# Two fused transformer blocks, float32: seven-product groups in another order, two weight sums on VectorE, eight plain tiles first

## The chip, the core and the metric

The kernel runs on one core of a Trainium2 chip. The metric is device time in microseconds (us) of one launch. TensorE (PE in the profile) multiplies, VectorE (DVE) and ScalarE (ACT) do elementwise work, GpSimd (POOL) does elementwise work and issues the transfers that add into memory, SyncE (SP) issues the plain transfers. Each engine takes its own instructions strictly in program order.

## What is computed

Two blocks over 512 tokens of width 2048, with 16 meta tokens ahead of them in the first. All is float32. The part that the change touches is the first product of block 1:

```python
def hybrid_layer(x, gain, w_in, pool_w, pool_scale, w_attn_up, w_pool_up, w_out):
    h = rmsnorm(x, gain)
    zin = h @ w_in
    q, k, v, g_attn, u, g_pool, m_attn, m_pool = split(zin)
    ...
    merged = sigmoid(m_attn) * y_attn + sigmoid(m_pool) * y_pool
    return x + merged @ w_out
```

m_attn and m_pool are 32 tiles of 128 columns (tiles 48 to 79 of w_in). Their sigmoids are computed first of all and parked in DRAM (`smd`). Only these 32 tiles change their computation; everything after them (attention, pooling, the second block with two layers) keeps its instructions and their order on every engine.

## The kernel before

**Arithmetic.** Every float32 operand is split in a high part (a rounding copy) and a low part (the rest): weights in `wh` (a cast on ACT, L195) and `wl` (a subtraction on DVE, L196), activations in `xh`, `xl`. A product takes three matmuls: xh·wh, xl·wh, xh·wl.

**Weights.** A chunk is 128 x 1024 float32 (512 KB), loaded by SP into one of five `ws` buffers. `ahead` casts and subtracts chunks in a fixed sequence of jobs, always three chunks ahead of the one that TensorE is about to use: `chunk`, at the start of every body, emits the split of job c+3, and only then do the matmuls of job c and their evacuation follow. That is the order on ACT and DVE: the split of a job three places ahead stands in front of the evacuation of the present one.

**Plain tiles.** The first NP = 6 of the 32 tiles are computed as they are: two chunks and 48 matmuls of 512 columns each. Meanwhile two generators work beside them: `sums` (the RMS norm) and `build`. `build` makes, for each of eight pairs j of activation tiles, the differences that the groups need: two scalings on ACT (`xt`, L538), one subtraction on POOL and four small operations on DVE (`sa`, `sb`), then two splits (`sh` on ACT, `sl` on DVE). The numbers in its `yield 0, delay, 0` say after how many planned ns its next part may be emitted. Whatever is not emitted when the plain tiles end is emitted at once (`need`). Evacuating a plain tile is a scaling (`p`), a clamp (`sg`) on DVE, and three activations on ACT (the sigmoid).

**Groups.** The other 26 tiles go in 13 groups of two. A group has four weight blocks: b11 and b21 are the two halves (over the 2048 inputs) of its first tile, b12 and b22 those of its second. With sums of them and of the activations it takes seven products of 24 matmuls of 256 columns, where two plain tiles take 96 of 512 columns. The products are named p1, p2, q5, p3, p6, p7, q4. Four weight blocks are loaded; four further operands are made by adding a block from DRAM into a loaded buffer with a transfer that POOL issues (L173, `accum_op=ALU.add`): q5 and p6 and q4 add b12, b22, b21 one after the other into the buffer T1 of p1, each after the split that reads the buffer, and p7 adds b22 into its own. The products of two groups are interleaved; with ' for the group before, the order is p1 p7' p2 q5 q4' p3 p6. Each product accumulates into one of three PSUM regions: a (p1, p2), c (q5, p3), b (p6, p7, q4). After p1 its partial sum is copied out (`after1`, ACT L278), and so on; `after6`, `after7`, `after4` read region b on DVE, and the next product into b must wait for them. `after7` and `after4` end in a clamp on DVE and the three sigmoid activations on ACT.

Of the kernel before, what the change touches and what calls it, by code (L numbers as in the profile page):

```python
# [9 lines left out]
ALU = mybir.AluOpType  # L10
# [36 lines left out]
class Unit:  # L47
    def __init__(self, chunks, body):
        self.chunks = chunks
        self.body = body  # L50


class Job:

    def __init__(self, load=None, src=None, acc=None, last=True, half=False):
        self.load, self.src, self.acc, self.last, self.half = load, src, acc, last, half
        self.tile = None
        self.w = (load if load is not None else acc).shape[-1]  # L60


class Group:
# [6 lines left out]
class K:  # L70
# [61 lines left out]
    def run(self, plan):  # L132
        plan = self.expand(plan)
        self.jobs = []
        for u in plan:
            if isinstance(u, Unit):
                for c in u.chunks:
                    if not isinstance(c, Job):
                        c = Job(load=c[0], half=True) if isinstance(c, tuple) else Job(load=c)
                    self.jobs.append(c)  # L140
        self.ci = self.si = self.di = self.ai = self.raw = 0
        self.split_w = {}
        for u in plan:
            if isinstance(u, Unit):
                for cost in u.body():
                    self.clock += cost
                    self.poll()
            else:
                u()
        self.need(*list(self.gens))  # L150
# [12 lines left out]
                    self.nc.sync.dma_start(t[:, a:b], j.load[:, a:b])  # L163
            self.di += 1

    def add(self, n):

        while self.ai < min(n, self.di):
            j = self.jobs[self.ai]
            if j.acc is not None:  # L170
                if j.src is not None:
                    j.tile = j.src.tile
                self.nc.gpsimd.dma_start(j.tile[:, :j.w], j.acc, accum_op=ALU.add)  # L173
            self.ai += 1

    def ahead(self, n):
        n = min(n, len(self.jobs))
        while self.si < n:
            self.fetch(self.si + 1)
            self.add(self.si + 1)  # L180
            j = self.jobs[self.si]
            t, w = j.tile, j.w
            h = self.wp.tile([P, CH], F32R, tag="wh", bufs=H_BUFS, name="wh")
            if j.half:

                h3 = h.rearrange("p (k c) -> p k c", c=P)
                t3 = t[:, :w].rearrange("p (k c) -> p k c", c=64)
                self.nc.scalar.copy(h3[:, :, :64], t3)
                self.nc.vector.tensor_tensor(h3[:, :, 64:], t3, h3[:, :, :64].bitcast(F32), ALU.subtract)
                l = None  # L190
            else:
                l = self.wp.tile([P, CH], F32R, tag="wl", bufs=L_BUFS, name="wl")
                cuts = [0, 256, w] if self.si == 0 else [0, w]
                for a, b in zip(cuts, cuts[1:]):
                    self.nc.scalar.copy(h[:, a:b], t[:, a:b])  # L195
                    self.nc.vector.tensor_tensor(l[:, a:b], t[:, a:b], h[:, a:b].bitcast(F32), ALU.subtract)  # L196
                    if self.si == 0 and a == 0:
                        self.first()
            self.split_w[self.si] = (h, l)
            if j.last:  # L200
                self.raw -= 1
            self.si += 1
            self.add(self.si + 2)

    def chunk(self):
        self.ahead(self.ci + 1 + AHEAD)
# [6 lines left out]
    def expand(self, plan):  # L213

        out, left, mid = [], [], []
        for n, u in enumerate(plan):
            if isinstance(u, Group):
                p1, p2, q5, p3, p6, p7, q4 = self.products(u)
                l7, l4 = left or ([], [])
                out += [p1, *l7, *mid, p2, q5, *l4, p3, p6]  # L220
                left, mid = [[p7], [q4]], []
            elif left and isinstance(u, Unit) and n + 1 < len(plan) and isinstance(plan[n + 1], Group):
                mid.append(u)
            elif left:
                out += left[0] + [u] + left[1] if isinstance(u, Unit) else left[0] + left[1] + [u]
                left = []
            else:
                out.append(u)
        return out + [x for l in left for x in l]

    def products(self, g):
# [5 lines left out]
        nc = self.nc  # L237
        b11, b21, b12, b22 = g.b
        st = {}
        lo, mid, hi = g.cols  # L240
        lom = lo - g.meta
        job = {"p1": Job(load=b11, last=False), "p2": Job(load=b21), "p3": Job(load=b22), "p7": Job(load=b12, acc=b22)}
        job["q5"] = Job(src=job["p1"], acc=b12, last=False)
        job["p6"] = Job(src=job["p1"], acc=b22, last=False)
        job["q4"] = Job(src=job["p1"], acc=b21)

        def product(key, op, region, first, after):
            cols = slice(lom if key in ("p1", "p2", "p3", "p6") else lo, mid)
# [23 lines left out]
        wide, half = slice(0, mid - lom), slice(lo - lom, mid - lom)  # L272
        one, two = slice(lom, mid), slice(mid, hi)
        first_half = slice(lo, mid)

        def after1(a):
            st["s"], st["v"], st["y0"], st["y1"] = self.U("s15"), self.U("vw"), self.U("y0"), self.U("y1")
            nc.scalar.copy(st["s"][:, one], a[:, wide])  # L278

        def after2(a):  # L280
# [3 lines left out]
            nc.scalar.copy(st["s"][:, two], c[:, half])  # L284

        def after6(b):
            v = st["v"]
            nc.vector.tensor_tensor(v[:, one], b[:, wide], st["s"][:, one], ALU.add)  # L288
            nc.vector.tensor_tensor(st["y1"][:, one], st["c"][:, wide], v[:, one], ALU.subtract)

        def after7(b):
            v, s = st["v"], st["s"]
            nc.vector.tensor_tensor(v[:, two], b[:, half], s[:, first_half], ALU.add)
            nc.vector.tensor_tensor(st["y1"][:, two], s[:, two], v[:, two], ALU.subtract)
            g.evacs[1](st["y1"])

        def after4(b):
# [1 line left out]
            g.evacs[0](st["y0"])  # L299

        return (product("p1", "A11", "a", True, after1), product("p2", "A12", "a", False, after2),
                product("q5", "S1", "c", True, after5), product("p3", "S4", "c", False, lambda c: None),
                product("p6", "S2", "b", True, after6), product("p7", "S3", "b", False, after7),
                product("q4", "A22", "b", False, after4))

# [174 lines left out]
    def block1(self, plan):  # L480
        nc, i = self.nc, self.i
        self.X = [None] * KT
        st = {}
# [49 lines left out]
        def build(xts):  # L533

            for j in range(KT // 2):
                x0, x1 = xts[2 * j], xts[2 * j + 1]
                for n, x in ((0, x0), (1, x1)):
                    nc.scalar.activation(x[:, :NT], x[:, :NT], AF.Copy, scale=self.vcol(V_NG, 2 * j + n))  # L538
                yield 0, 900, 0
                a, b = self.U("sa"), self.U("sb")  # L540
                nc.vector.tensor_tensor(a[:, HALF:NT], x0[:, HALF:NT], x1[:, HALF:NT], ALU.subtract)
                nc.gpsimd.tensor_tensor(b[:, HALF:NT], x0[:, META:HALF], x0[:, HALF:NT], ALU.subtract)
                nc.vector.tensor_scalar(a[:, :META], x0[:, :META], -1.0, None, ALU.mult)
                nc.vector.tensor_tensor(a[:, META:HALF], a[:, HALF:NT], x0[:, META:HALF], ALU.subtract)
                nc.vector.tensor_tensor(b[:, :HALF], x1[:, :HALF], a[:, :HALF], ALU.add)
                yield 0, 1500, 0
                r = []
                for t in (a, b):
                    h, l = self.UR("sh"), self.UR("sl")
# [1 line left out]
                    r.append((h, l))  # L551
                X0, X1 = self.X[2 * j], self.X[2 * j + 1]
                self.XS.append({"A11": X0, "A12": X1, "A22": X1, "S1": r[0], "S2": r[0], "S3": r[1], "S4": r[1]})
                yield 0, 2000, 0

        X = self.X
        XS = self.XS = []
# [109 lines left out]

            return Unit(chunks, body)

        NP = 6  # L670
        plan.append(load)
        plan.append(self.pair_unit([wt(48), wt(49)], X, [ev_m(0), ev_m(1)], lo=META, kts=EVEN_ODD))
        for n in range(2, NP):
# [910 lines left out]
```

## Time and profile before

| | us or share |
|---|---|
| median of 3 runs (2726.71 to 2731.55) | 2729.45 |
| the profiled execution, whole | 2726.03 |
| its span, first to last instruction | 2724.3 |
| plain tiles: start to the first group's first matmul | 6.67 to 79.32 |
| 13 groups: to the first matmul of the next stage | 79.32 to 383.59 |
| TensorE's share of the chain that ended last | 88% |

The profile gives busy times of the engines, a chain of work traced back from the end, groups of instructions with their durations and what ended the idle time before them, and, for a stretch, the granted TensorE clock (1.00 is 2.4 GHz, 0.50 is 1.2 GHz). A matmul's end is modelled, so the start times of consecutive matmuls say more than the busy share.

### The profile page before, as it was taken

What the parts mean: (1) busy time and instruction counts of PE and PEld (TensorE: products, weight loads), DVE (VectorE), ACT (ScalarE), POOL (GpSimd) and SP (SyncE); (2) the same over time, 40 slices, a digit from 0 to 9 for tenths busy, and PEclk for the clock granted to TensorE, in tenths of its full rate; (3) what the DMA queues carried; (4) which work ended last, traced back from release to release, by engine and by line L of the source; (5) the groups of instructions that cost most, each with busy time, mean ns of one, the idle gap of its engine ahead of it and who ended that gap; (6) DMA issues with size and microseconds to landing.
All of it is one profiled execution on the core that took longest, in us unless ns stands there. A gap on an engine that the chain in (4) does not pass through costs nothing.

```text
span 2724.3 us, 36840 instructions
## 1 busy us (share of the span) xinstructions
PE 2663.6 (98%) x14558; PEld 2299.0 (84%) x14558; DVE 1465.9 (54%) x2057; ACT 1181.9 (43%) x2074; POOL 552.9 (20%) x625
## 2 busy tenths in 40 slices
PE   8699989999999999999999999999999999999997
PEld 7699989889999888888888888888888888888886
DVE  7555554444444443544466665366555666546734
ACT  6555543444444322234345554344344555334433
POOL 2111101112112220002202231133320223112223
PEclk9899999999999999999999999999999999999998
DMA  5599962222222234444432223233342222332322
GB/s 195 132 219 232 229 175 86 78 78 81 81 71 82 86 116 142 139 136 139 141 107 70 78 78 97 84 107 93 105 145 90 78 78 78 98 96 84 106 93 70
DMA packets 100285, 304.78 MB, mean 112 GB/s; under 512 B 10896, under 2 KB 15376, under 8 KB 100112
## 3 DMA queue, kind: packets, MB, share of 16 engines
q1 hardware_dynamic: 90448, 273.06, 30.9%
q0 software_dynamic: 7488, 27.27, 5.7%
q8 instruction: 114, 1.87, 0.3%
q10 hardware_dynamic: 2176, 2.10, 0.2%
q14 instruction: 59, 0.48, 0.1%
HBM read 281.41 MB, written 20.97 MB: 111 GB/s over the span
## 4 chain that ended last, share of the span: by engine, by line
PE 88%; DMA 3%; DVE 3%; ACT 3%; issue 1%; POOL 0%; DVEq 0%; SPq 0%; ACTq 0%; POOLq 0%
PE pm L332 75%; DMA ws<-w_in 3%; PE s L1441 2%; ACT wh L195 2%; DVE wl L196 1%; PE o L1495 1%; PE o L1411 1%; PE t L1388 1%; PE pm L263 1%; PE o L923 1%; PE pm L264 1%; PE pm L265 1%; PE z L880 1%; PE t L1477 1%; PE s L1355 1%
## 5 line engine op out<-in xcount | busy, mean ns | idle before, releaser
L196 DVE TENSOR_TENSOR wl<-ws,wh 128x1024 fp32r<-128x1024 f32 (+2 forms) x480 | 622.3, 1302 | 472.7 <-ACT wh L195 467.8
L332 PE MATMUL pm<-xh,wh 128*128 128x512 f32 (+1 forms) x2240 | 742.3, 359 | 7.4 <-ACT xh L503 7.4
L332 PE MATMUL pm<-xl,wh 128*128 128x512 f32 (+1 forms) x2240 | 736.2, 357 | 0.2 <-DVE xl L504 0.2
L332 PE MATMUL pm<-xh,wl 128*128 128x512 f32 (+1 forms) x2240 | 735.8, 356 | 0.0
L195 ACT CAST wh<-ws 128x1024 fp32r<-128x1024 f32 (+2 forms) x480 | 491.6, 1028 | 384.7 <-PE pm L332 246.2
L332 PEld LDWEIGHTS pm<-xh,wh 128*128 128x128 f32 x2240 | 398.5, 188 | 69.2 <-ACT xh L503 8.1
L332 PEld LDWEIGHTS pm<-xh,wl 128*128 128x128 f32 x2240 | 396.4, 188 | 64.3
L332 PEld LDWEIGHTS pm<-xl,wh 128*128 128x128 f32 x2240 | 395.8, 188 | 59.2 <-DVE xl L504 1.3
L332 PE MATMUL pm<-yh,wh 128*128 128x512 f32 (+1 forms) x544 | 207.9, 382 | 0.0
L332 PE MATMUL pm<-yl,wh 128*128 128x512 f32 (+1 forms) x544 | 206.7, 380 | 0.0
L332 PE MATMUL pm<-yh,wl 128*128 128x512 f32 (+1 forms) x544 | 206.6, 380 | 0.0
L443 ACT ACTIVATE sg<-sg 128x512 f32<-128x512 f32 x80 | 50.5, 632 | 278.3 <-DVE sg L442 278.3
L263 PE MATMUL pm<-sh,wh 128*128 128x256 f32 x416 | 119.0, 286 | 15.0 <-DVE vw L288 9.4
L332 PEld LDWEIGHTS pm<-yh,wl 128*128 128x128 f32 x544 | 102.1, 188 | 21.0
L332 PEld LDWEIGHTS pm<-yl,wh 128*128 128x128 f32 x544 | 102.3, 188 | 19.6
L332 PEld LDWEIGHTS pm<-yh,wh 128*128 128x128 f32 x544 | 102.2, 188 | 19.7
L264 PE MATMUL pm<-sl,wh 128*128 128x256 f32 x416 | 117.7, 283 | 0.0
L265 PE MATMUL pm<-sh,wl 128*128 128x256 f32 x416 | 117.4, 282 | 0.0
L263 PE MATMUL pm<-xh,wh 128*128 128x256 f32 x312 | 88.8, 285 | 22.6 <-ACT s L278 22.0
L1004 POOL TENSOR_TENSOR gs<-p,sg 128x512 f32<-128x512 f32 x32 | 41.6, 1301 | 293.7 <-ACT sg L445 259.3
L332 PE MATMUL pm<-mh,wl 128*128 128x512 f32 x256 | 101.0, 395 | 0.0
L332 PE MATMUL pm<-mh,wh 128*128 128x512 f32 x256 | 100.9, 394 | 0.0
(336 smaller groups left out, 4505.0 us busy)
## 6 DMA issues: line engine op xcount, KB each, us to landing
ws<-w_in SPq DMA_DIRECT2D x283, 512.0 KB, 3.7
ws<-w_out SPq DMA_DIRECT2D x96, 512.0 KB, 3.9
ws<-w_in POOLq DMA_DIRECT2D x52, 512.0 KB, 7.0
smd<-sg SPq DMA_DIRECT2D x32, 256.0 KB, 5.2
ws<-w_au SPq DMA_DIRECT2D x16, 512.0 KB, 3.6
sm<-smd SPq DMA_DIRECT2D x32, 256.0 KB, 3.9
ws<-w_pu SPq DMA_DIRECT2D x16, 512.0 KB, 3.5
xr<-xs SPq DMA_DIRECT2D x32, 256.0 KB, 4.3
```

The costliest lines, as they stand in the source:

```text
L195: self.nc.scalar.copy(h[:, a:b], t[:, a:b])
L196: self.nc.vector.tensor_tensor(l[:, a:b], t[:, a:b], h[:, a:b].bitcast(F32), ALU.subtract)
L263: mm(o, wh[:, sl], xh, start=first and n == 0, stop=False, skip_group_check=True)
L264: mm(o, wh[:, sl], xl, start=False, stop=False, skip_group_check=True)
L265: mm(o, wl[:, sl], xh, start=False, stop=n == nj - 1, skip_group_check=True)
L332: mm(ps, w[:, sl], x[:, lo:hi], start=s, stop=e)
L443: nc.scalar.activation(e[:, :n], e[:, :n], AF.Exp, scale=-1.0)
L880: mm(o[:nb, lo:lo + ZW[b2]], lhs, t[x], start=False, stop=b2 == b and x == 1, skip_group_check=True)
L923: mm(o[:, ZC0[b]:S], vv, am[b][y], start=n == 0 and b == 0, stop=n == 2 and b == 4, skip_group_check=True)
L1004: nc.gpsimd.tensor_tensor(gs[:, :S], p[:, :S], e[:, :S], ALU.mult)
L1355: mm(o, q, kk[0][:, k0:k0 + 256], start=True, stop=False)
L1441: mm(o, p[:, q], r[:, :w], start=x == 0, stop=x == 4)
```

## The change

The order of a group's products becomes p1 p7' p2 q4' q5 p6 p3. Loads are now four (b11 for p1, b21 for p2, b22 in T6 and b12 in T3, which the jobs p6 and p3 fetch). Two sums remain with POOL's transfers: b12 into T1 after p1's split (for q5), b21 into T1 after p6's split (for q4). Two are now additions on DVE (128 x 1024 float32): T1 += T6 after q5's split (for p6), T3 += T6 after p6's split (for p7). `after6` and `after3` write into y1 instead of a buffer of their own. NP becomes 8, so there are 12 groups. `build` yields shorter delays.

```diff
@@ ahead @@
-            self.fetch(self.si + 1)
-            self.add(self.si + 1)
             j = self.jobs[self.si]
-            t, w = j.tile, j.w
+            self.fetch(self.si + 1 + 2 * bool(j.after))
+            t, w = j.src.tile, j.w
...
-            if j.last:
-                self.raw -= 1
+            self.raw -= len(j.frees)
+            for x, y in j.after:
+                if isinstance(y, Job):
+                    self.nc.vector.tensor_tensor(x.tile[:, :w], x.tile[:, :w], y.tile[:, :w], ALU.add)
+                else:
+                    self.nc.gpsimd.dma_start(x.tile[:, :w], y, accum_op=ALU.add)
             self.si += 1
-            self.add(self.si + 2)
@@ expand @@
-                out += [p1, *l7, *mid, p2, q5, *l4, p3, p6]
+                out += [p1, *l7, *mid, p2, *l4, q5, p6, p3]
@@ products @@
-        job = {"p1": Job(load=b11, last=False), "p2": Job(load=b21), "p3": Job(load=b22), "p7": Job(load=b12, acc=b22)}
-        job["q5"] = Job(src=job["p1"], acc=b12, last=False)
-        job["p6"] = Job(src=job["p1"], acc=b22, last=False)
-        job["q4"] = Job(src=job["p1"], acc=b21)
+        p1, p2, p6, p3 = Job(load=b11), Job(load=b21), Job(load=b22), Job(load=b12)
+        q5, p7, q4 = Job(src=p1), Job(src=p3, frees=(p3,)), Job(src=p1, frees=(p1,))
+        p2.frees = (p2,)
+        p3.frees = (p6,)
+        p6.src, p3.src = p1, p6
+        p1.after = ((p1, b12),)
+        q5.after = ((p1, p6),)
+        p6.after = ((p1, b21), (p3, p6))
...
         def after6(b):
-            v = st["v"]
-            nc.vector.tensor_tensor(v[:, one], b[:, wide], st["s"][:, one], ALU.add)
-            nc.vector.tensor_tensor(st["y1"][:, one], st["c"][:, wide], v[:, one], ALU.subtract)
+            v = st["y1"][:, one]
+            nc.vector.tensor_tensor(v, b[:, wide], st["s"][:, one], ALU.add)
+
+        def after3(c):
+            v = st["y1"][:, one]
+            nc.vector.tensor_tensor(v, c[:, wide], v, ALU.subtract)
@@ build @@
-                yield 0, 900, 0
+                yield 0, 600, 0
...
-                yield 0, 1500, 0
+                yield 0, 900, 0
...
-                yield 0, 2000, 0
+                yield 0, 900, 0
...
-        NP = 6
+        NP = 8
```

On ACT, in the plain stage, from the cast of chunk 10 (the first of tile 5) to that of chunk 11; `xt` and `sh` are of `build`, `sg` is the sigmoid of a tile. Before:

```order
L195 CAST wh<-ws 128x1024
L318 CAST sh<-sa 128x528
L318 CAST sh<-sb 128x528
L538 ACTIVATE xt<-xt,vec 128x528 x2
L443 ACTIVATE sg<-sg 128x512
L444 ACTIVATE sg<-sg 128x512
L445 ACTIVATE sg<-sg 128x512
L195 CAST wh<-ws 128x1024
```

After the change, the same place:

```order
L187 CAST wh<-ws 128x1024
L321 CAST sh<-sa 128x528
L321 CAST sh<-sb 128x528
L541 ACTIVATE xt<-xt,vec 128x528 x2
L321 CAST sh<-sa 128x528
L321 CAST sh<-sb 128x528
L446 ACTIVATE sg<-sg 128x512
L447 ACTIVATE sg<-sg 128x512
L448 ACTIVATE sg<-sg 128x512
L187 CAST wh<-ws 128x1024
```

One more pair of `build`'s splits stands between two weight casts.

On DVE, one group from `after7` on (L293 or L296 is its first line, L298 or L301 the first of `after4`). Before:

```order
L196 TENSOR_TENSOR wl<-ws,wh 128x1024 x2
L293 TENSOR_TENSOR vw<-pm,s_1024 128x256
L294 TENSOR_TENSOR y_1027<-s_1024,vw 128x256
L622 TENSOR_TENSOR y_1027<-y_1027,rsb 128x512
L442 TENSOR_SCALAR sg<-y_1027 128x512
L196 TENSOR_TENSOR wl<-ws,wh 128x1024 x3
L298 TENSOR_TENSOR y_1026<-pm,s_1024 128x256
L622 TENSOR_TENSOR y_1026<-y_1026,rsb 128x512
L442 TENSOR_SCALAR sg<-y_1026 128x512
```

After the change (the first `wl` row holds q4' and q5 of the next group; then `ws<-ws` is T1 += T6):

```order
L188 TENSOR_TENSOR wl<-ws,wh 128x1024 x2
L195 TENSOR_TENSOR ws<-ws 128x1024
L296 TENSOR_TENSOR y_1005<-pm,s_1003 128x256
L297 TENSOR_TENSOR y_1005<-s_1003,y_1005 128x256
L625 TENSOR_TENSOR y_1005<-y_1005,rsb 128x512
L445 TENSOR_SCALAR sg<-y_1005 128x512
L188 TENSOR_TENSOR wl<-ws,wh 128x1024
L195 TENSOR_TENSOR ws<-ws 128x1024
L188 TENSOR_TENSOR wl<-ws,wh 128x1024
L301 TENSOR_TENSOR y_1004<-pm,s_1003 128x256
L625 TENSOR_TENSOR y_1004<-y_1004,rsb 128x512
L445 TENSOR_SCALAR sg<-y_1004 128x512
```

Before, `after7` stood behind the split of q4', and the three splits after it were of p3, p6 and the next p1. Now it stands behind the split of q5 and an addition, the splits after it are of p6 and p3, and that of the next p1 comes after `after4`.

On ACT, the same stretch (L281 and L284 are `after2` and `after5`). Before, from the sigmoid of `after7` on:

```order
L443 ACTIVATE sg<-sg 128x512
L444 ACTIVATE sg<-sg 128x512
L445 ACTIVATE sg<-sg 128x512
L195 CAST wh<-ws 128x1024
L281 COPY y_1026<-pm 128x256
L195 CAST wh<-ws 128x1024
L284 COPY s_1024<-pm 128x256
L195 CAST wh<-ws 128x1024
L443 ACTIVATE sg<-sg 128x512
L444 ACTIVATE sg<-sg 128x512
L445 ACTIVATE sg<-sg 128x512
L195 CAST wh<-ws 128x1024 x3
```

After the change, the casts are of q5, p6, p3 and the next p1:

```order
L187 CAST wh<-ws 128x1024
L446 ACTIVATE sg<-sg 128x512
L447 ACTIVATE sg<-sg 128x512
L448 ACTIVATE sg<-sg 128x512
L187 CAST wh<-ws 128x1024
L281 COPY y_1162<-pm 128x256
L187 CAST wh<-ws 128x1024
L446 ACTIVATE sg<-sg 128x512
L447 ACTIVATE sg<-sg 128x512
L448 ACTIVATE sg<-sg 128x512
L187 CAST wh<-ws 128x1024
```

The cast of the next p1 stood ahead of the sigmoid of `after4`; now it stands behind it.

## Rows read from the trace of the kernel before

**Rows 1.** TensorE by stretch: start:end, length, busy (matmuls), clock, DMA share, GB/s.

```profile
68.28:79.32 11.04, 11.04 (x50) 1.00 0.37 93
79.32:104.31 24.99, 2.99 (x25) 0.63 0.46 104
104.31:118.80 14.49, 14.03 (x96) 0.82 0.55 113
118.80:347.69 228.89, 221.60 (x1850) 1.00 0.91 225
187.83:201.99 14.16, 14.16 (x123) 1.00 0.89 223
347.69:383.59 35.90, 28.04 (x219) 0.90 0.77 205
```

**Rows 2.** Timeline of TensorE: start, length, instruction, [idle before it, what ended it].

```profile
104.31 0.58 PE L263 MATMUL pm<-xh,wh 128*128 128x256 f32 x1 [22.00 <-ACT s L278]
...
375.19 0.55 PE L263 MATMUL pm<-sh,wh 128*128 128x256 f32 x1 [6.78 <-DVE vw L288]
```

**Rows 3.** The chain of waits in the group stage: start, length, what.

```profile
134.58 9.79 DMA ws<-w_in
...
144.39 1.06 ACT wh L195
...
145.48 1.23 DVE wl L196
...
150.59 1.03 ACT wh L195
...
154.09 1.24 DVE wl L196
...
155.61 0.54 POOL ws L173
156.15 10.46 DMA ws<-w_in
```

**Rows 4.** Timeline of VectorE: `after7`'s and `after4`'s first operations.

```profile
146.62 0.42 DVE L293 TENSOR_TENSOR vw<-pm,s 128x256 f32<-128x256 f32 x1
...
155.23 0.42 DVE L298 TENSOR_TENSOR y<-pm,s 128x256 f32<-128x256 f32 x1
```

**Rows 5.** Timeline of ScalarE: the casts behind the sigmoid of that `after4`.

```profile
158.82 1.99 ACT L195 CAST wh<-ws 128x1024 fp32r<-128x1024 f32 x2
```

**Rows 6.** The page, part 6: plain weight loads, KB each, median us to landing.

```profile
ws<-w_in SPq DMA_DIRECT2D x283, 512.0 KB, 3.7
```

**Rows 7.** Line L173 from 70 to 105 us: three adding transfers, one at a time.

```profile
DMA to landing us min/median/max: 5.6/5.6/5.8
```

**Rows 8.** DMA issues from 143.8 to 145 us: one adding transfer, plain loads beside it.

```profile
ws<-w_in POOLq DMA_DIRECT2D x1, 512.0 KB, 6.6
```

**Rows 9.** Timeline of ScalarE in the plain stage: casts of weights, `build`'s scalings.

```profile
61.71 1.03 ACT L195 CAST wh<-ws 128x1024 fp32r<-128x1024 f32 x1
...
70.02 1.03 ACT L195 CAST wh<-ws 128x1024 fp32r<-128x1024 f32 x1
...
96.19 1.36 ACT L538 ACTIVATE xt<-xt,vec 128x528 f32<-128x528 f32 x2
...
99.57 1.36 ACT L538 ACTIVATE xt<-xt,vec 128x528 f32<-128x528 f32 x2
```

**Rows 10.** Timeline of VectorE in the plain stage.

```profile
45.28 0.41 DVE L541 TENSOR_TENSOR sa<-xt 128x256 f32<-128x256 f32 x1
...
46.55 0.76 DVE L423 TENSOR_SCALAR ms<-pms 128x264 f32<-128x264 f32 x2
...
66.97 0.68 DVE L616 TENSOR_TENSOR p<-pm,rsb 128x512 f32<-128x512 f32 x1
...
76.40 1.62 DVE L545 TENSOR_TENSOR sb<-xt,sa 128x272 f32<-128x272 f32 x1
```

**Rows 11.** Timeline of GpSimd in the same place: `build`'s subtraction.

```profile
76.71 1.00 POOL L542 TENSOR_TENSOR sb<-xt 128x256 f32<-128x256 f32 x1
```

More of the change, by code (lines that the diff above doesn't have):

```diff
@@ L53, with __init__ @@
 class Job:
-    def __init__(self, load=None, src=None, acc=None, last=True, half=False):
-        self.load, self.src, self.acc, self.last, self.half = load, src, acc, last, half
+    def __init__(self, load=None, src=None, frees=(), half=False):
+        self.load, self.src, self.frees, self.half = load, src or self, frees, half
+        self.after = ()
         self.tile = None
-        self.w = (load if load is not None else acc).shape[-1]
+        self.w = load.shape[-1] if load is not None else src.w
 class Group:
@@ L139, in run @@
                         c = Job(load=c[0], half=True) if isinstance(c, tuple) else Job(load=c)
+                        c.frees = (c,)
                     self.jobs.append(c)
-        self.ci = self.si = self.di = self.ai = self.raw = 0
+        self.ci = self.si = self.di = self.raw = 0
         self.split_w = {}
@@ L164, in fetch @@
             self.di += 1
[L166 to L174, printed above, removed]
     def ahead(self, n):
@@ L241, in products @@
         lom = lo - g.meta
[L242 to L245 removed]
+        p1, p2, p6, p3 = Job(load=b11), Job(load=b21), Job(load=b22), Job(load=b12)
[6 more added lines that the diff above has]
+        p6.after = ((p1, b21), (p3, p6))
+        job = {"p1": p1, "p2": p2, "p3": p3, "q5": q5, "p6": p6, "p7": p7, "q4": q4}
         def product(key, op, region, first, after):
@@ L276, in after1 @@
         def after1(a):
-            st["s"], st["v"], st["y0"], st["y1"] = self.U("s15"), self.U("vw"), self.U("y0"), self.U("y1")
+            st["s"], st["y0"], st["y1"] = self.U("s15"), self.U("y0"), self.U("y1")
             nc.scalar.copy(st["s"][:, one], a[:, wide])
@@ L286, in after6 @@
         def after6(b):
-            v = st["v"]
-            nc.vector.tensor_tensor(v[:, one], b[:, wide], st["s"][:, one], ALU.add)
-            nc.vector.tensor_tensor(st["y1"][:, one], st["c"][:, wide], v[:, one], ALU.subtract)
+            v = st["y1"][:, one]
[3 more added lines that the diff above has]
+            nc.vector.tensor_tensor(v, c[:, wide], v, ALU.subtract)
         def after7(b):
-            v, s = st["v"], st["s"]
-            nc.vector.tensor_tensor(v[:, two], b[:, half], s[:, first_half], ALU.add)
-            nc.vector.tensor_tensor(st["y1"][:, two], s[:, two], v[:, two], ALU.subtract)
+            s, w = st["s"], st["y1"][:, two]
+            nc.vector.tensor_tensor(w, b[:, half], s[:, first_half], ALU.add)
+            nc.vector.tensor_tensor(w, s[:, two], w, ALU.subtract)
             g.evacs[1](st["y1"])
@@ L301, in products @@
         return (product("p1", "A11", "a", True, after1), product("p2", "A12", "a", False, after2),
-                product("q5", "S1", "c", True, after5), product("p3", "S4", "c", False, lambda c: None),
+                product("q5", "S1", "c", True, after5), product("p3", "S4", "c", False, after3),
                 product("p6", "S2", "b", True, after6), product("p7", "S3", "b", False, after7),
```

## The prediction

> **What bounds the kernel now.** Most of the chain that ended last is TensorE, so only places where TensorE waits can pay. The stretches of TensorE show where [rows 1]. Plain tiles run without a gap, 11.04 us a tile. The first group's first product then ends in a wait of 22.0 us [rows 2], and the clock falls with it (0.63 in that stretch, 0.82 in the next). In the group stage five products without a stall take 14.16 us, so 2.83 a product and 19.8 a group of seven; eleven groups (118.80 to 347.69) take 228.89 us, 20.8 each. So 1.0 us a group is lost. At the tail there is one more wait of 6.8 us [rows 2]. From 383.59 on nothing changes: the rest of the program keeps its order on all engines. So I forecast when the next stage begins, 383.59 now.
>
> With no wait at all it would begin at 79.32 + 2 x 11.04 + 84 x 2.83 = 339.1, that is 44.5 us earlier. Whether it does hangs on what makes the waits.
>
> The 22 us come from `build`: what is not emitted when the plain tiles end stands on ACT ahead of `after1` (L278), and p2 needs that. The waits of the group stage come from a **ring**, which the chain shows [rows 3]: an adding transfer lands, the cast (1.06 to 1.09 with its handover) and the low part of q4's weights follow, then `after7` on DVE [rows 4], its sigmoid, three casts, the low part of the next p1, and 0.28 us after that POOL issues the next adding transfers. From 134.58 to 156.15 that is 21.57 us, of which 9.79 are the transfer and 11.8 all else. The transfer takes so long because two are issued back to back (155.61, 156.15) and the critical one is the second: 9.8 and 10.5 us, where one alone takes 5.6 to 5.8 [rows 7], and one beside plain loads 6.6 [rows 8].
>
> **The change: transfers and additions.** Two of four adding transfers go, and the two that stay are issued by different splits (after p1 and after p6), never back to back. I take D = 5.9 us for one: the row alone is 5.6, the row beside loads 6.6, and the new stage has fewer bytes than the old one. Range 5.5 to 6.6. An addition on DVE is not in the trace; the nearest row is the low part, also two 1024-wide float32 inputs in SBUF, 1.23 us, and 1.14 from its start to the next one's [rows 3, 4]. I take 1.14, and 1.27 for T1 += T6, which waits for the low part just before it. A gain is excluded (work is added), more than 1.3 too.
>
> **The change: the ring that the new order makes.** The order rows show that `after7` now stands on DVE behind q5's split and the first addition, and q5's split waits for the transfer after p1's split. They also show that the casts of p6, p3 and the next p1 now stand behind *two* sigmoids, those of `after7` and `after4`, where before the next p1 stood behind one. So the ring from one p1 split to the next is:
> transfer 0.28 + 5.9; cast of q5 and handover 1.11; low part 1.27; addition 1.14; that is 9.7 to the start of `after7`. From there to the next cast, 3.97 (146.62 to 150.59) [rows 3, 4]; that cast, of p6, to its low part 1.07; low part of p6, addition, low part of p3, 3 x 1.14 = 3.42; `after4` to the cast behind its sigmoid, 3.59 (155.23 to 158.82) [rows 4, 5]; cast of p1 1.07 and low part 1.23. Sum 9.7 + 3.97 + 1.07 + 3.42 + 3.59 + 2.30 = **24.05 us**.
> That is longer than TensorE's 19.8 and than the 20.8 of now. The shorter transfer (-4) is paid for by one more sigmoid (3.6), two additions and a low part more in the ring. TensorE does not enter it: q4' ends 3.3 us after `after7` starts, and `after4` is only reached 8.5 us after it.
>
> **The change: plain tiles and `build`.** Two plain tiles take the place of a group: 22.1 us of TensorE for 19.8. What counts for the ring is when p1's first block (chunk 16) is split. The cast of chunk 10 is at 61.71 now [rows 9]. In the new order four things have moved ahead of it in the two queues: a pair of low parts before the norm (twice 0.68, by the row of 512 columns), one scaling pair before the cast of chunk 9 (1.36), `build`'s four DVE operations before the inverse root (1.27, from 45.28 to 46.55), another scaling pair (1.36) [rows 9, 10]; so about 67.1. From there to the cast of chunk 16 ACT and DVE pass, one behind the other, six build steps of 3.38 (96.19 to 99.57), three evacuations of 3.05 (66.97 to 70.02) [rows 9, 10], six casts of 1.0 [rows 5], and some 2 us of low parts in between: 20.3 + 9.2 + 6 + 2 = 37.5. So the cast at 104.6, the split done 2.3 later at 106.9. On this way the casts of chunks 11 and 13 come some 3 us after TensorE wants them, each with a low part behind it: 8 to 9 us of waits in the plain stage take the place of the 22.0 (and of 2.4 us of low clock) after it. From 103, if part of an evacuation lies beside a build step, to 110, if four steps meet POOL's subtraction as the row of 1.62 us does [rows 10, 11].
>
> That row is where a rule bears. Of the Trainium skill, the page SBUF — State Buffer, section "SBUF: two separate sides", says that DVE with two SBUF inputs and a GpSimd operation that reads SBUF lock each other out for a whole instruction. The 1.62 us (76.40 to 78.02), with POOL's operation in the middle of it (76.71 to 77.71), agrees; by the rule each of the six steps could lose 1.2 us, 114.1 in place of 106.9, and without it none.
>
> **The sum.** Split of the first p1 done 106.9. To that of the second p1: 9.7 to the addition's end, 3.05 for the evacuation of the last plain tile, then 1.07 + 3.42 + 1.23: 18.5. Ten further rings: 240.5. From there 9.7 to the last `after7` but one, and the tail: 3.97 + 1.07 + 3.42 + 3.59 to the cast of p7's sum, 2.2 to the low part of q4, 1.6 until `after6` behind it is done, then p7 (2.83), `after7` (0.6) and q4 (2.83): 22.1. Together 106.9 + 18.5 + 240.5 + 9.7 + 22.1 = **397.7**, that is 14.1 us later than 383.59. On the profiled execution, 2726.0, that is 2740.1; on the median of the runs shown, which lies 3.4 higher, 2743.5. I say **2741**.
>
> D counts twelve times: 5.5 gives -5, 6.6 gives +8. The first split gives -4 to +3. So the next stage begins at 389 to 409, or +5 to +26: 2731 to 2757 over the spread of the runs before.
>
> **Rivals.**
> *The transfer shrinks (faster).* With half as many of them, an adding transfer might come near a plain load, 3.7 us [rows 6]. Then twelve times 2.2 us go: 371.3, 12.3 us earlier than now, 2714 to 2717. The point of balance is D = 4.7. Against it: with nothing beside it, the row says 5.6. Its sibling is that the ring doesn't close at all and TensorE sets the pace, 339, so 2682 to 2685; against that stands the order, which closes it. Together 0.10.
> *It comes out even.* Short D and an early first split together (389), or a DVE step or two that overlap: within 0.2% of before, which is about what a measurement here can tell from no change. 2726 to 2734. 0.08.
> *The clock falls in the group stage.* TensorE would now wait some 4 us a group in three pieces (1.7 before q4', the rest at p1). The old stage held 1.00 with 1.0 a group; the stretches with 22 and 6.8 us of waiting show 0.63 and 0.90 [rows 1]. If it fell once a group, a product would cost up to 2.4 us more, as p2 did after the 22 us; where the ring has no room, twelve times, 29: 2768 to 2772. The Trainium skill says this too: the page TensorE: Matmul & The Clock Gate, section "HAM oscillation — how this bites in real kernels", describes kernels that fall back to 1.2 GHz at every wait for data. The trace bears it out for the long waits alone. 0.07.
>
> **Chances and range.** Forecast 0.75, faster rivals 0.10, even 0.08, clock 0.07. The range 2724 to 2758 takes in the forecast's own and the even case, and leaves out the rest. Faster by over 0.2% 0.10, within 0.2% 0.08, slower 0.82.
>
> **What would show it.** Right: twelve groups at some 24 us each; p2's 22 us wait gone, waits of some 3 us at two chunks of the plain stage; waits before q4' (for `after7`) and before p1 in each group; single adding transfers of 5.5 to 6.6 us; a chain through transfer, q5's cast, the addition, `after7`, p6's cast, `after4`, p1's cast. Wrong: groups of 20 us, with DVE's low parts done ahead; or adding transfers near 4 us; or a granted clock below 1.00 in the stage.

## The result, and the profile after

The changed kernel takes **2769.24 us** (median of 4 runs, 2766.30 to 2769.99), the kernel before 2730.34 beside it: ratio 1.0143, 95% interval 1.0125 to 1.0160, slower by 39 us. The forecast was 2741, 11 us slower, with a range of 2724 to 2758. The direction was right; the time lies outside the range.

The profiled execution has a span of 2767.0 us, 42.7 more than before. The next stage begins at 427.15 instead of 383.59, 43.6 later, so all of the loss lies where the prediction looked. Lines of the page (engines: busy, share, instructions; DMA issues, count, KB, median us to landing):

```profile
PE 2688.0 (97%) x14486; PEld 2318.1 (84%) x14486; DVE 1486.0 (54%) x2073; ACT 1177.8 (43%) x2068; POOL 526.8 (19%) x597
ws<-w_in POOLq DMA_DIRECT2D x24, 512.0 KB, 5.7
```

The adding transfers are half as many, and their median is 5.7 us. The stretches that answer to [rows 1] (start:end, length, busy times of the engines, granted clock, DMA share, GB/s): the first group, ten groups, the tail, and two single p3.

```profile
113.62:136.41 22.79, 16.18 (x122) 15.98 (x120) 11.07 (x11) 8.77 (x12) 1.73 (x2) 0.85 0.52 124
136.41:393.21 256.80, 220.49 (x1683) 217.82 (x1682) 148.39 (x180) 114.59 (x160) 17.28 (x20) 0.91 0.55 143
393.21:427.15 33.94, 28.79 (x217) 28.21 (x217) 18.46 (x24) 13.85 (x20) 0.87 (x1) 0.90 0.56 160
...
156.48:160.60 4.12, 4.12 (x25) 4.12 (x26) 3.62 (x4) 1.84 (x2) 0.86 (x1) 0.68 0.94 189
...
308.76:314.05 5.29, 5.29 (x25) 5.29 (x26) 3.62 (x4) 1.84 (x2) 0.86 (x1) 0.50 0.91 197
```

Ten groups take 256.80 us, 25.7 each; the group stage of before had 20.8 [rows 1]. The clock, which was 1.00 there, is 0.91, and that is at one place of a group, p3 and what lies beside it: p3 begins at 0.50, or falls to it within its first 1.6 us, and takes 4.1 to 5.3 us instead of 2.83. With the start of p1, which runs at 0.50 in some groups too, the low clock costs 1.5 to 2.9 us a group, 2.0 on average. TensorE's longest sum of waits (us, times, longest), and two waits on its timeline, which answer to [rows 2]:

```profile
PE pm L263 <- ACT s L284: 38.8, 11, 4.1
```

```profile
123.21 0.58 PE L263 MATMUL pm<-xh,wh 128*128 128x256 f32 x1 [6.61 <-ACT s L278]
...
308.76 0.58 PE L263 MATMUL pm<-sh,wh 128*128 128x256 f32 x1 [4.05 <-ACT s L284]
```

The 22.0 us in front of p2 are down to 6.6. But in each of eleven groups p3 waits 3 to 4 us, and what it waits for is `after5`'s copy of region c (L284), a wait that the forecast did not have at all. ScalarE's timeline ahead of that p3 says why:

```profile
305.55 0.63 ACT L446 ACTIVATE sg<-sg 128x512 f32<-128x512 f32 x1 [3.87 <-DVE sg L445]
...
307.41 1.03 ACT L187 CAST wh<-ws 128x1024 fp32r<-128x1024 f32 x1
308.34 0.36 ACT L284 COPY s<-pm 128x256 f32<-128x256 f32 x1
```

The copy stands behind the sigmoid of `after4` and the cast of the next p1. Before, it stood ahead of that sigmoid, as the order rows of before show; in the order rows of after it is missing only because they end one row ahead of it.

The chain of waits through one group, which answers to [rows 3, 4]:

```profile
317.35 0.13 PE pm L265
...
317.50 0.02 ACT s L278
...
317.77 1.06 ACT wh L187
318.85 1.24 DVE wl L188
320.11 1.23 DVE ws L195
321.34 0.34 DVE y L296
...
325.22 1.04 ACT wh L187
...
327.42 1.22 DVE ws L195
328.64 1.14 DVE wl L188
329.77 0.35 DVE y L301
...
333.19 1.04 ACT wh L187
334.25 1.24 DVE wl L188
...
335.77 8.95 DMA ws<-w_in
```

From 317.77 on that is the forecast ring, step by step: cast, low part and addition of q5, `after7`, cast of p6, addition, low part of p3, `after4`, cast and low part of p1, transfer. From 317.77 to 335.77 it is 18.0, forecast 18.15 without the transfer. The transfer is not: 8.95 where 5.9 were put in. The first two rows show that this group was not started by a transfer: its q5 was cast when p1 had ended on TensorE and `after1`'s copy (L278), which stands ahead of that cast on ScalarE, was done. All 22 adding transfers from 124.46 us on (shortest, median and longest time to landing):

```profile
DMA to landing us min/median/max: 5.5/5.7/9.3
```

The b21 ones, with no weight load beside them but in the first, take 5.5 to 6.2. Of the b12 ones, which are on the ring, the ten in the rings take 5.5 to 9.0, 7.0 on average. Two plain loads start 0.95 and 2.4 us behind all but the first of them, in buffers that the two splits behind p1's (p7' and p2) have just given back. The DMA issues beside a long one (335.77) and beside a short one (258.50), with the same starts:

```profile
ws<-w_in SPq DMA_DIRECT2D x2, 512.0 KB, 8.0
ws<-w_in POOLq DMA_DIRECT2D x1, 512.0 KB, 8.9
...
ws<-w_in SPq DMA_DIRECT2D x2, 512.0 KB, 7.3
ws<-w_in POOLq DMA_DIRECT2D x1, 512.0 KB, 5.6
```

So there were three suspects in the group stage: the transfer's own length; a second ring that goes through TensorE (sigmoid of `after4`, cast of p1, `after5`'s copy, p3, p1, and through `after1`'s copy, or a weight buffer that p1 gives back, to q5's split); and the fallen clock. The rest of the loss lies in the plain stage, where the waits moved.

### The profile page after: what moved, and what is told of

Same layout as the page of the kernel before. It is cut to its first block, busy times and chain, and to the rows that moved or that the text cites. A ratio compares the mean times of both kernels' runs of the same rounds, so it can differ in the third digit from the quotient of the medians.

```text
span 2767.0 us, 36637 instructions
## 1 busy us (share of the span) xinstructions
PE 2688.0 (97%) x14486; PEld 2318.1 (84%) x14486; DVE 1486.0 (54%) x2073; ACT 1177.8 (43%) x2068; POOL 526.8 (19%) x597
## 4 chain that ended last, share of the span: by engine, by line
PE 87%; DVE 5%; ACT 3%; DMA 2%; issue 2%; DVEq 0%; POOL 0%; SPq 0%; ACTq 0%; POOLq 0%
PE pm L335 74%; DMA ws<-w_in 2%; PE s L1444 2%; DVE wl L188 1%; ACT wh L187 1%; PE o L1498 1%; PE o L1414 1%; DVE ws L195 1%; PE pm L263 1%; PE t L1391 1%; PE pm L264 1%; PE pm L265 1%; PE o L926 1%; PE z L883 1%; ACT sg L447 1%
## 5 line engine op out<-in xcount | busy, mean ns | idle before, releaser
L188 DVE TENSOR_TENSOR wl<-ws,wh 128x1024 fp32r<-128x1024 f32 (+3 forms) x477 | 619.2, 1302 | 484.9 <-ACT wh L187 478.6
L335 PE MATMUL pm<-xh,wh 128*128 128x512 f32 (+1 forms) x2272 | 755.8, 360 | 13.8 <-ACT xh L506 8.1
L335 PE MATMUL pm<-xh,wl 128*128 128x512 f32 (+1 forms) x2272 | 750.6, 358 | 1.5 <-DVE wl L188 1.5
L335 PE MATMUL pm<-xl,wh 128*128 128x512 f32 (+1 forms) x2272 | 749.9, 358 | 0.2 <-DVE xl L507 0.2
L187 ACT CAST wh<-ws 128x1024 fp32r<-128x1024 f32 (+3 forms) x477 | 488.1, 1027 | 389.3 <-PE pm L335 246.0
L335 PEld LDWEIGHTS pm<-xh,wh 128*128 128x128 f32 x2272 | 405.6, 189 | 77.5 <-ACT xh L506 8.8
L335 PEld LDWEIGHTS pm<-xh,wl 128*128 128x128 f32 x2272 | 403.0, 189 | 68.4 <-DVE wl L188 2.8
L335 PEld LDWEIGHTS pm<-xl,wh 128*128 128x128 f32 x2272 | 402.5, 189 | 61.1 <-DVE xl L507 1.3
L446 ACT ACTIVATE sg<-sg 128x512 f32<-128x512 f32 x80 | 50.5, 631 | 297.7 <-DVE sg L445 297.7
L263 PE MATMUL pm<-sh,wh 128*128 128x256 f32 x384 | 118.8, 309 | 38.8 <-ACT s L284 38.8
L263 PEld LDWEIGHTS pm<-sh,wh 128*128 128x128 f32 x384 | 81.8, 213 | 41.0 <-ACT s L284 41.0
L335 PE MATMUL pm<-ml,wh 128*128 128x512 f32 x256 | 100.8, 394 | 0.0
```

What stands on the lines that cost most here:

```text
L263: mm(o, wh[:, sl], xh, start=first and n == 0, stop=False, skip_group_check=True)
L335: mm(ps, w[:, sl], x[:, lo:hi], start=s, stop=e)
L446: nc.scalar.activation(e[:, :n], e[:, :n], AF.Exp, scale=-1.0)
```

## The experiments

**Plain tiles, delays and order apart.** Two kernels take the parts one by one. The first keeps the groups of before.

```diff
-                yield 0, 900, 0
+                yield 0, 600, 0
...
-                yield 0, 1500, 0
+                yield 0, 900, 0
...
-                yield 0, 2000, 0
+                yield 0, 900, 0
...
-        NP = 6
+        NP = 8
```

> The kernel before with eight plain tiles first and the shorter delays of build, its groups untouched. Theory A (the loss lies in the new order of the groups): the plain stage ends as in the changed kernel, with p1 at about 113.6 us, and twelve groups at the old 20.8 us follow; the next stage begins at 375 to 381 us, 2 to 9 us earlier than before, ratio 0.997 to 0.999. Theory B (the eight plain tiles and the denser build bring the loss): slower than before, by up to 30 us.

Measured 2724.72, ratio 0.9989 (0.9979 to 0.9998), as theory A expected.

The second has the new groups alone: the changed kernel with the delays and the tiles of before.

```diff
-                yield 0, 600, 0
+                yield 0, 900, 0
...
-                yield 0, 900, 0
+                yield 0, 1500, 0
...
-                yield 0, 900, 0
+                yield 0, 2000, 0
...
-        NP = 8
+        NP = 6
```

> The changed groups with six plain tiles and the delays of before. Theory A: 13 groups of some 25.8 us instead of 20.8, about 60 us slower than before, ratio 1.02, since the 22 us wait stays as well. Theory B: near the time of before.

Measured 2786.4, ratio 1.0210 (1.0193 to 1.0227). So the new groups cost 57 us where there are 13 of them, and 44.5 where there are 12 (2769.24 less 2724.72). The rest of the change gives 3 us back with the old groups, and 17 with the new ones, of which it leaves one out.

**Only the place of one sigmoid.** The changed kernel, in which `after4` with its clamp and sigmoid is emitted one product later, behind `after5`; nothing else moves.

```diff
         def after5(c):
             nc.scalar.copy(st["s"][:, two], c[:, half])
+            for f in self.late:
+                f()
+            self.late = []
...
         def after4(b):
-            nc.vector.tensor_tensor(st["y0"][:, two], b[:, half], st["s"][:, first_half], ALU.add)
-            g.evacs[0](st["y0"])
+            def f():
+                nc.vector.tensor_tensor(st["y0"][:, two], b[:, half], st["s"][:, first_half], ALU.add)
+                g.evacs[0](st["y0"])
+
+            if g.final:
+                f()
+            else:
+                self.late.append(f)
```

> The changed kernel, but after4 with its sigmoid is emitted one product later, behind after5, so that neither p1's cast nor after5's copy on ScalarE stands behind that sigmoid. Theory A (p3 waits for after5's copy behind that sigmoid, the clock falls, and the ring passes through TensorE): groups fall from 25.8 to 20 to 21 us, the 3.1 us wait before p3 goes, the clock stays at 1.00; 45 to 60 us faster than the changed kernel, so 2710 to 2725 us. Rival C (the adding transfer of 6 to 9 us sets the ring): the sigmoid counts for 3.6 us of the ring as well, but groups stay at 22 us or more where the transfer takes 8 to 9 us: 2730 to 2745 us. Rival D (the clock alone): no change beyond 10 us.

Measured 2728.95, ratio 0.9999 (0.9990 to 1.0008): 40 us below the changed kernel, as fast as the one before, and between the two ranges expected. Ten groups and one transfer of the chain:

```profile
136.22:349.54 213.32, 201.95 (x1683) 199.05 (x1681) 143.25 (x177) 110.33 (x157) 17.27 (x20) 1.00 0.63 167
```

```profile
239.64 8.39 DMA ws<-w_in
...
261.49 7.63 DMA ws<-w_in
```

A group takes 21.3 us, the clock is 1.00, and p3's wait is gone. The transfer has become longer still, since b12's is now issued 3.4 us behind b21's; the ring is shorter all the same, because the sigmoid and p1's cast behind it have left it. From 239.64 to 261.49 it is 21.85, of which 13.46 are not the transfer, against 18.1 before: the sigmoid's place costs 4.6 a ring. It was in the forecast's sum, with 3.59 and 1.07 for the cast behind it. The move takes the sigmoid out of both rings at once, so this run doesn't part them.

**Is the clock the cause?** The changed kernel with 24 matmuls between p6 and p3 whose result nobody reads. They keep TensorE at work while p3 waits.

```diff
+                if key == "p3":
+                    scratch = self.bank("pm")
+                    for n in range(nj):
+                        xh, xl = g.X[n][op]
+                        sl = slice(n * P, n * P + P)
+                        for wd, x in ((wh, xh), (wh, xl), (wl, xh)):
+                            mm(scratch[:, :mid - lom], wd[:, sl], x[:, cols], start=True, stop=True, skip_group_check=True)
```

> The changed kernel, with 24 matmuls more in each group, into a bank that nobody reads, between p6 and p3, where TensorE waits 3.1 us for after5's copy. They add 2.83 us of work a group. Theory A with the clock as a part of it: p3 then runs at the full clock, 2.83 us instead of about 5, and a group takes 1 to 2 us less: 10 to 25 us faster than the changed kernel in spite of the added work. Rival C (transfers alone): no change, or slower by up to 30 us.

Measured 2770.23, ratio 1.0151 (1.0136 to 1.0166), the time of the changed kernel. Nine groups, one transfer of the chain with the next one, and all transfers:

```profile
160.12:393.59 233.47, 211.45 (x1730) 208.94 (x1730) 132.79 (x163) 103.76 (x145) 15.54 (x18) 0.98 0.55 143
```

```profile
212.73 8.66 DMA ws<-w_in
...
239.48 8.54 DMA ws<-w_in
```

```profile
DMA to landing us min/median/max: 5.3/5.6/9.6
```

The mean clock of the span rises from 0.985 to 0.993 and p3 takes 2.8 to 2.9 us, but nothing is gained. Each ring is now 18.1 us and the transfer: 26.75 from 212.73 to 239.48, with 8.66. So with the clock back in p3 the ring through TensorE sets no group any more. The expectation missed because the b12 transfers came out longer in this kernel (7.85 on average in these nine rings, 7.17 in the same ones of the changed kernel), which takes back what the shorter TensorE ring gives, some 6 us. That the clock costs nothing is therefore not shown; what is shown is that it alone does not make the loss.

**Without the transfer on the ring.** The changed kernel with b12 loaded plainly (as p6's block) and added to T1 on VectorE; b21 remains a transfer.

```diff
-            self.fetch(self.si + 1 + 2 * bool(j.after))
+            self.fetch(self.si + 1 + 5 * bool(j.after))
...
-        p1, p2, p6, p3 = Job(load=b11), Job(load=b21), Job(load=b22), Job(load=b12)
+        p1, p2, p6, p3 = Job(load=b11), Job(load=b21), Job(load=b12), Job(load=b22)
...
-        p1.after = ((p1, b12),)
-        q5.after = ((p1, p6),)
-        p6.after = ((p1, b21), (p3, p6))
+        p1.after = ((p1, p6),)
+        q5.after = ((p1, p3),)
+        p6.after = ((p1, b21), (p6, p3))
```

> The changed kernel with a third sum on VectorE: b12, which is loaded anyway, is added to T1 there after p1's split (1.27 us) in place of the adding transfer of 5.5 to 9.3 us; one adding transfer a group stays, off the ring. Theory A (two rings lie beside each other: one through the transfer, 18.15 us plus the transfer, and one through TensorE, p3 behind after5's copy, p1, and the weight buffer that q5's cast needs, 24.4 to 25.3 us): the first shrinks to some 19 us, the second stays, groups of 24 to 25.3 us instead of 25.8; 2744 to 2757 us. Rival C (only the transfer counts): groups of 20 us, 2700 to 2712 us.

Measured 2756.41, ratio 1.0096 (1.0081 to 1.0111). Nine groups, and p3's wait in one:

```profile
157.09:381.96 224.87, 196.22 (x1514) 194.21 (x1513) 142.76 (x172) 102.69 (x144) 7.77 (x9) 0.92 0.47 127
```

```profile
228.56 0.58 PE L263 MATMUL pm<-sh,wh 128*128 128x256 f32 x1 [2.94 <-ACT s L284]
```

A group still takes 25.0 us, with p3's wait and the clock at 0.92. So the ring through TensorE alone, without any transfer on it, is longer than the 24.05 of the forecast ring. That is with the fallen clock in it: the low clock costs 1.8 us a group on average here, and without it the group would be 23.2, an estimate, below the 24.05.

**What makes the transfer long?** The kernel with the 24 extra products, in which the three loads that start behind the b12 transfer are held back until q5's cast, which waits for it.

```diff
+                    if self.touch:
+                        self.nc.scalar.copy(t[:, a:a + 1], self.vcol(V_NG, 0))
                     self.nc.sync.dma_start(t[:, a:b], j.load[:, a:b])
...
-            self.fetch(self.si + 1 + 2 * bool(j.after))
+            self.fetch(self.si + 1 + sum(isinstance(y, Job) and 1 + (x is not j.src) for x, y in j.after))
...
                 if isinstance(y, Job):
+                    if x is j.src:
+                        self.wait, self.touch = False, True
...
                     self.nc.gpsimd.dma_start(x.tile[:, :w], y, accum_op=ALU.add)
+                    self.wait |= x is j
...
-        self.fetch(self.si + STAGE_BUFS)
+        if not self.wait:
+            self.fetch(self.si + STAGE_BUFS)
+            self.touch = False
```

The copy of one column, which the load overwrites, stands on ScalarE behind q5's cast.

> The changed kernel with 24 unread products in front of p3 (e4), in which the three plain loads of a group that are issued within 4 us after the b12 transfer are held back until q5's cast, which waits for that transfer; nothing is left out. Theory: the b12 transfer takes 5.6 us alone and up to 9.6 us only because of these loads, so all of them fall to 5.4 to 5.9 us, a group of 18.1 us + transfer to 23.5 to 24.0 us, and the kernel from 2770 to 2745 to 2756 us. Rival: the transfer's length does not come from these loads: still 5.9 to 9.6 us, and 2766 to 2775 us.

Measured 2750.83, ratio 1.0084 (1.0064 to 1.0103), as expected and 19 us below the same kernel without it. Nine groups and all transfers:

```profile
159.29:376.71 217.42, 206.70 (x1730) 204.28 (x1730) 132.78 (x163) 106.24 (x172) 15.54 (x19) 1.00 0.60 153
```

```profile
DMA to landing us min/median/max: 5.3/5.6/7.2
```

A group falls from 25.9 to 24.16 us; the nine b12 transfers average 6.06, and each ring is again 18.1 and its transfer, within 0.02. They were expected at 5.9 at most. Three took 6.5 to 7.2, though no load starts behind them and the one 2.0 us ahead of them is also ahead of those that took 5.4; why is open. So the loads behind the transfer make most of what it takes above 5.5 us, not all.

**Both cures together.** The two edits above, `after4` behind `after5` and b12 added on VectorE:

```diff
+                self.late.append(f)
...
+        p1.after = ((p1, p6),)
+        q5.after = ((p1, p3),)
```

> The changed kernel with after4 one product later and the b12 sum on VectorE. Theory A: no ring is longer than TensorE's own 19.8 us a group (14.5 without transfer and second sigmoid); groups of 19.8 to 20.2 us, the next stage begins at 362 to 369 us, 2705 to 2714 us, faster than the kernel before. Rival (VectorE, with three additions a group, becomes the bound): groups over 21 us, 2725 us or more.

Measured 2776.16, ratio 1.0171 (1.0156 to 1.0186): slower than the changed kernel, where 2705 to 2714 were expected. The chain shows a new ring:

```profile
229.44 1.23 DVE wl L190
230.68 5.28 DMA ws<-w_in
236.06 1.23 DVE ws L197
237.28 0.34 DVE y L307
```

The plain load of b12 starts only when p3's low part (229.44) gives a buffer back, and the addition of b12 at 236.06 waits for it, with `after4` (L307) right behind it on VectorE. A sixth load buffer, paid for with two of the 75 activation buffers, takes that wait away:

```diff
-STAGE_BUFS = 5
+STAGE_BUFS = 6
...
-U_BUFS = 75
+U_BUFS = 73
```

> The late-sigmoid kernel with b12 added on VectorE (e8), with six weight buffers for loads instead of five and 73 instead of 75 activation buffers. Theory: e8 lost its time because b12 could only start loading when p3's split gave a buffer back, 6 us before the addition that p7's cast stands behind; with a sixth buffer the load starts earlier, that wait goes, no adding transfer is left on a ring, and a group should need 20 to 20.8 us: 2710 to 2722 us. Rival: the addition in VectorE's queue in front of the steps after p7 costs the time by itself: stays over 2745 us.

Measured 2725.63, ratio 0.9990 (0.9980 to 0.9999): 50.5 us less, so the missing buffer was the cause of that loss. It stays 4 us above the expected range. Its chain, in one group:

```profile
248.00 1.23 DVE wl L190
249.25 1.22 DVE ws L197
...
254.36 1.04 ACT wh L189
...
257.70 2.37 DVE wl L190 x2
260.09 1.22 DVE ws L197
...
264.74 1.04 ACT wh L189
...
269.87 1.23 DVE wl L190
```

From 248.00 to 269.87 it is 21.9 us with no transfer in it: casts, low parts, additions and two sigmoids, one behind the other on two engines. That is the next limit behind both of those found.

**A faster kernel.** Delays and plain tiles once more, with the groups of before: first the short delays alone.

```diff
-                yield 0, 900, 0
+                yield 0, 600, 0
...
-                yield 0, 1500, 0
+                yield 0, 900, 0
...
-                yield 0, 2000, 0
+                yield 0, 900, 0
```

> The kernel before with build's shorter delays alone, six plain tiles. Theory A: the casts of chunks 10 to 13 come late, p1 starts at some 86 us instead of 79, p2 at 100 to 104 instead of 104.3: 0 to 5 us faster than before. Rival (dense delays cost the 10 us that they cost in the plain stage): 5 to 10 us slower.

Measured 2729.16, ratio 0.9996 (0.9987 to 1.0006): nothing. Then the eight plain tiles alone.

```diff
-        NP = 6
+        NP = 8
```

> The kernel before with eight plain tiles, build's old delays and the old groups. Theory A: build, spread over six and a half planned us a step, ends before the plain tiles do and doesn't hold the weight casts up; p2 follows p1 within some 5 us, twelve groups at 20.8 us: 8 to 18 us faster than before, 2710 to 2720 us. Rival (the eight tiles themselves cost what they hide): 2724 to 2730 us, like the run with the dense delays.

Measured **2718.37**, ratio 0.9959 (0.9945 to 0.9973), the lowest median of all here, and faster than both kernels. Its plain stage:

```profile
47.86:103.28 55.42, 55.42 (x242) 45.19 (x241) 39.13 (x67) 36.59 (x56) 8.71 (x8) 1.00 0.29 95
103.28:120.00 16.72, 5.81 (x38) 5.60 (x37) 8.74 (x15) 9.08 (x13) 2.47 (x3) 0.68 0.79 168
```

Ten chunks run without a gap; then TensorE waits for what is left of `build`, but 11 us instead of 22.0 [rows 2]. With the short delays as well (2724.72) the same work stands in front of the casts of chunks 10 to 13, and 6 us of the gain go. The same holds for the kernel with the late sigmoid, when the delays of before are put back:

```diff
-                yield 0, 600, 0
+                yield 0, 900, 0
...
-                yield 0, 900, 0
+                yield 0, 1500, 0
...
-                yield 0, 900, 0
+                yield 0, 2000, 0
```

> The late-sigmoid kernel (e3) with the three longer delays of the kernel before for the activation sums (0.9, 1.5 and 2.0 us of the planner's clock). Theory: beside eight plain tiles the short delays cost what they cost in the kernel before's groups (2724.7 against 2718.4 us), since the sums crowd VectorE and ScalarE in front of the casts of chunks 10 to 13: 2720 to 2725 us. Rival: they cost nothing here: 2727 to 2731 us.

Measured 2720.78, ratio 0.9971 (0.9961 to 0.9981), 8 us below the same with short delays; its interval and that of 2718.37 overlap. With the same edit the kernel with six buffers gains less:

> e9 (late sigmoid, b12 added on VectorE, six buffers for loads) with the longer delays of e10. If the load wait and the delays both count and lie in different stages, both gains add: 2704 to 2717 us. If e9's sixth buffer does not help, over 2738 us.

Measured 2724.01, ratio 0.9985 (0.9976 to 0.9995): 1.6 us below, the gains do not add. With the old delays the waits in the plain stage go, but p2's wait grows from 5.9 to 13.4 us (from 6.8 to 12.1 in the pair before), which takes most of it back; the rest is open.

## Why the prediction was right in direction and wrong in size

Of the 29.45 us by which the next stage came later than the forecast 397.7, the first split gives 1.2, the first ring 4.1, the ten further rings 17.65 and the tail 6.5.

**The plain stage: right.** The casts of the first blocks of tiles and the first split, which answer to [rows 9]:

```profile
67.33 1.04 ACT L187 CAST wh<-ws 128x1024 fp32r<-128x1024 f32 x1
...
77.53 1.03 ACT L187 CAST wh<-ws 128x1024 fp32r<-128x1024 f32 x1
...
93.49 1.03 ACT L187 CAST wh<-ws 128x1024 fp32r<-128x1024 f32 x1
```

```profile
79.85 0.83 DVE L544 TENSOR_TENSOR sa<-xt 128x256 f32<-128x256 f32 x1
...
105.78 2.36 DVE L188 TENSOR_TENSOR wl<-ws,wh 128x1024 fp32r<-128x1024 f32 x2 [2.96 <-ACT wh L187]
```

Chunk 10 is cast at 67.33 (forecast 67.1), chunks 11 and 13 come late as forecast, and the split is done at 108.14 (106.9). The waits and the low clock behind them take 11.6 us of TensorE's time there, forecast 8 to 9. The Trainium skill's rule of the lock (SBUF — State Buffer, section "SBUF: two separate sides") would have given 114.1; the trace agrees with it in kind only. The operation at 79.85 lies beside POOL's subtraction and takes 0.83 instead of 0.42, another 0.95, and a low part 1.25 instead of 0.70; the other three of the six subtractions cost VectorE 0.1 us or nothing. In the row that the forecast took (1.62 us) VectorE's operation starts 0.3 us ahead of POOL's by the profile and yet is the longer one by all of it; by the page the first to start holds the lock, so that row shows only that the two met.

**The first ring: a step left out.** Forecast 18.5, measured 22.6. The sum went through the transfer, the addition and the evacuation of the last plain tile. But `after1`'s copy stands behind that sigmoid and p6's cast too, so p2 waited 6.6 us, which the forecast had as gone, and began at the low clock, and p1's cast waited for `after2` of that late p2. Another 0.9 are the transfer.

**The ring: right.** The held-back kernel, in which the second ring is gone, has nine rings of 24.16 us; the forecast was 24.05. The list of its steps, with 1.14 for an addition, held to 0.1 us in all.

**The term D: mis-sized.** It was taken as 5.9, from 5.5 to 6.6, by the one row of a transfer beside loads [rows 8]. In the ten rings it was 7.0 on average, which is 11 us of the 17.65, and in the tail 9.28, which is 3.4 of the 6.5. That row was of a transfer with one plain load 2.8 us and another adding transfer 3.8 us behind it; the prediction saw that fewer bytes move in the new stage, but not when the loads would be issued, though the same list of freed buffers tells it.

**"TensorE does not enter it": wrong.** What stands behind that sentence looks at q4' and `after4`, not at `after5`. Its copy now stands behind the sigmoid of `after4`; p3 needs the copy, p1 follows p3, and q5's split needs the end of p1. With b12 on VectorE this ring sets 25.0 a group. In the changed kernel five of the ten rings were 18.05 and their transfer, and the other five, with transfers of 5.5 to 6.2, were longer than that, by some 7 us in all. In the first of these (3.1 us) the late p2 still told; in the other four TensorE's ring was 0.2 to 1.8 us the longer one, in each by less than the low clock cost there (1.5 to 2.9). In the tail p3 waited for the same copy and ran at the low clock, which is some 2.7 of the 3.1 us left. That both rings hang on one place is shown by the kernel with the late sigmoid: 25.7 to 21.3 a group by moving that alone.

**The rivals.** The clock did fall once a group, and cost 1.5 to 2.9 us, where up to 2.4 were priced. The time of that rival, 2768 to 2772, is the one measured, but by luck: its 29 us were twelve falls, and longer transfers alone make 15 of the 29.45. The fallen clock is a part of the second ring, and by the figures of the last paragraph, as an estimate, that ring would have set only the first of its five groups at the full clock; the fill can't settle it, as its transfers grew. The page TensorE: Matmul & The Clock Gate of the Trainium skill, section "HAM oscillation — how this bites in real kernels", tells of kernels that fall to 1.2 GHz at waits for data; the trace agrees (after 3 to 4 us of waiting p3 begins at 0.50 in seven of eleven groups), but for the other four, where it falls 0.4 to 1.6 us into p3. The rivals in which the transfer shrinks to 3.7 or the ring does not close did not come: 5.3 us is the shortest of all.

Of what was to show the forecast right, the groups of over 24 us and the chain as told were there. The waits were not: 38.8 us of them stand before p3, and only 2.6 before q4' (for `after7`), none before p1; and the single transfers went up to 9.3. What was to show it wrong was there too: a clock below 1.00 in the stage.

## What to carry to other kernels

When an order changes, write out for each engine's queue what now stands in front of every copy that frees a PSUM region, not only in front of the step that is looked at: a ring that is ruled out at one place can close at another. A transfer's length is read with the issue times of its neighbours, which follow from the buffers that come free around it. Whether a fallen clock costs time is tested by giving TensorE work, but only if the other terms of the ring stay as they were; here the transfers grew with it.

## What was not expected of the hardware

An adding transfer of 512 KB took 5.3 to 5.8 us in nearly all places of the changed kernel and the one with the fill where no plain load started within 5 us behind it (once 6.2), and 5.6 to 9.6 with two or three plain loads of the same size that start 1 to 4 us *behind* it; held back, 5.4 to 7.2. One plain load 2.0 us behind it cost nothing in the late-sigmoid kernel (b21 there: 5.5 to 5.8). Why the same starts behind it cost one transfer nothing (5.6) and another 3 us and more is open. After waits of 3 to 4 us the granted clock was at 0.50 for 3 to 6 us in each of eleven groups, from the start of the next product or from up to 1.6 us into it, where the waits of 1 us a group of the kernel before left it at 1.00. One addition on VectorE takes what a low part takes, 1.22 us and 1.14 from start to start; what the sums cost is the place that they take in the queue, 1.14 us each in the ring.
